# A two-layer decoder trunk: the first units' weight transfers tied to rows of the output projection, the modulation's columns tied to the units, and another order of the start

## The chip, the cores and the metric

The kernel runs on one core of one Trainium2 chip. The metric is the device time of one execution, in microseconds (us), as the median of several runs. All data are float32; a matmul takes its operands as "fp32r" pieces, high and low part, and each product is made of three matmuls (high x high, high x low, low x high).

## What is computed

Cut to what matters here:

```python
for i in range(DEPTH):                                  # 2 layers
    mod = (c_act @ ada_w[i] + ada_b[i])[:, None, :]     # 6 x 1024 columns
    sh1, sc1, g1, sh2, sc2, g2 = jnp.split(mod, 6, axis=-1)
    h = rmsnorm(x, norm1_g[i]) * (1.0 + sc1) + sh1
    proj = h @ w_in[i]
    mix = three mixers of proj                          # state space, pooling, attention
    x = x + g1 * (mix @ w_out[i])
    h = rmsnorm(x, norm2_g[i]) * (1.0 + sc2) + sh2
    x = x + g2 * conv_ffn(h, ffn_up[i], ffn_conv_w[i], ffn_conv_b[i], ffn_down[i])
return rmsnorm(x, final_g)
```

`x` is 1024 positions x 1024 channels, the hidden width of the gated MLP is 2816. `rmsnorm` divides by the root of the mean square over the channels, so it needs the whole sum of squares ("the root") before anything behind it can be made.

## The kernel before, in words

The channels lie on the partitions: `x` is eight tiles of 128 channels x 1024 positions. A helper library for tiles assigns buffers and semaphores, and its scheduler writes down each engine's order of instructions: by priority (the order of the program) among what its own model of time holds to be ready. Each engine then runs its list in order, and so does each queue of transfers: SP and ACT issue plain ones, POOL those that add to their destination (`accum_op=ALU.add`). `after(ins, dep)` (line 78) adds an edge that only fixes the order; with `sync` it is a real wait.

**The start.** `START` (line 32) is a list written by hand, and `start` (line 276) does one entry after the other: `x` loads the residual, `c`, `h`, `w` load data for the scale, the shift and the first weights, `S` adds up squares on ACT and DVE, `C` makes the scale (sixteen matmuls of one row, then a small transpose), `R0` the root in columns (line 198: matmuls L203, then L176 to L180), `R1` its spread over the positions (L211) and a copy into `xrs`, `X` multiplies half of `x` by it, `H` makes columns of the shift on DVE (L308), `M` and `N` the normalised input in high and low parts. The first projection (`vproj`, L411 to L413) follows.

**The columns of the modulation.** `ada_col` (line 138) makes one column of 128 values: two loads of 128 x 512 on SP (L142) into a ring of two raw buffers, which also serves the weights, and two multiply-and-add-up instructions on DVE (L143). Twelve columns are called for in the channel mixer of layer 0, one behind each of the units 7 to 18, and the rest among the down projection.

**The output projection, second part.** `accum_last` (line 1233) walks over two halves of 512 positions. In each, for eight blocks `n` of 128 channels: twelve matmuls into `dn` (L232 to L234), `accum` adds the result to the residual on DVE (L1211, called a row here), `store` writes it out on ACT's queue (L894), `square_add` squares it on ACT (L186) and adds it to `acc`, on POOL for n < 7 and on DVE for n = 7 (L187). The weights of a block are loaded on SP (L267) and split by ACT and DVE in the first half; those of n > 3 (`wkeep`, L261 and L262) are kept for the second. Behind each half come the root (L203) and its spread (L211). The seven first products of the channel mixer (`begin`, px and pv, L969 to L971) follow the second half.

**The units.** The channel mixer's up projection is done by a scheme of seven products in place of eight for each of 22 units (`unit`). A unit needs weights and sums of weights: `prepare(f)` (line 1018) loads S1 to S4 and A22 on SP (L989), and adds to them by transfers on POOL (L1024): S1 += w, S3 += w, S2 += S1, S4 += S2. Units 0 and 1 are prepared ahead of `accum_last`: ten loads that wait for `group_last`, the last addition of the projection's first part. Their eight sums are kept in a list, and `sums` issues one in each of the program's steps of the second half. `finish(f)` makes the convolution, the gate and the product on DVE (L1137, L1178) and writes it out.

## Time and profile before

| | us |
|---|---|
| median of 3 runs (2285.11 to 2291.4) | 2290.52 |
| the profiled execution, its own time | 2287.57 |
| its span, first to last instruction | 2285.8 |
| PE busy in the span | 2225.1 |
| DVE busy | 1553.3 |
| ACT busy | 1057.5 |
| POOL busy | 243.4 |

The engines are PE (matmul; PEld is its load of weights), DVE (vector), ACT (scalar functions), POOL (general) and SP (which issues transfers). A busy PE need not be PE at full speed: the granted clock is a column of its own, PEclk. A row of a timeline gives start, length, engine, line, operation, out<-in by the program's names, shapes and, in brackets, the idle time of the engine ahead of it with what ended that.

### The profile page before, as it was taken

The numbers are of one execution on the slowest core, as the hardware profiler recorded it, in microseconds if no ns is written. First come the engines' busy times: TensorE is split into PE (matmuls) and PEld (weight loads), VectorE is DVE, ScalarE is ACT, GpSimd is POOL, SyncE is SP. The second block draws the span as 40 slices with busy tenths as digits, with TensorE's granted clock in tenths as the row PEclk, the third lists the DMA queues.
The fourth block names the chain that finished last, engine by engine and source line by source line (L and its number), as shares of the span: only waits on it lengthen the run. The fifth ranks groups of instructions, "written<-read, shape, count | busy, mean of one in ns | idle before, by whom it ended". The sixth has DMA issues, their size and how long they took to land. (4 is left out here: it accounts for less than half of the span.)

```text
span 2285.8 us, 29760 instructions
## 1 busy us (share of the span) xinstructions
PE 2225.1 (97%) x10472; PEld 1808.7 (79%) x10472; DVE 1553.3 (68%) x2712; ACT 1057.5 (46%) x1960; POOL 243.4 (11%) x308
## 2 busy tenths in 40 slices
PE   6999999999999999999999999998999999999998
PEld 4878877778788888788888888776888888878887
DVE  6467888588766667995564567775966666675446
ACT  5366664355454445312234667533645455442212
POOL 0210000231111110000001000003211111100000
PEclk9999999999999999999999999999999999999999
DMA  7452333658876776991133221236777777663112
GB/s 275 130 146 79 93 112 126 164 161 221 212 197 172 179 175 202 338 298 59 56 134 108 56 56 48 87 106 183 181 179 174 175 175 179 162 244 106 47 47 88
DMA packets 186229, 338.94 MB, mean 148 GB/s; under 512 B 28704, under 2 KB 44320, under 8 KB 186080
## 3 DMA queue, kind: packets, MB, share of 16 engines
q1 hardware_dynamic: 126144, 244.44, 32.8%
q0 software_dynamic: 30560, 61.56, 15.0%
q10 hardware_dynamic: 29376, 31.05, 4.1%
q8 instruction: 82, 1.34, 0.2%
q14 instruction: 67, 0.55, 0.1%
HBM read 265.93 MB, written 44.83 MB: 136 GB/s over the span
## 5 line engine op out<-in xcount | busy, mean ns | idle before, releaser
L161 ACT CAST whi<-wraw 128x512 fp32r<-128x512 f32 (+2 forms) x196 | 117.6, 602 | 394.6 <-PE dq L233 274.1
L232 PE MATMUL dq<-ah,whi 128*128 128x512 f32 x576 | 227.0, 394 | 1.8 <-DVE xd L1230 1.4
L233 PE MATMUL dq<-al,whi 128*128 128x512 f32 x576 | 226.8, 394 | 0.0
L234 PE MATMUL dq<-ah,wlo 128*128 128x512 f32 x576 | 226.0, 393 | 0.0
L161 ACT CAST whi<-S 128x512 fp32r<-128x512 f32 x176 | 108.7, 619 | 206.9 <-PE px L970 129.0
L162 DVE TENSOR_TENSOR wlo<-wraw,whi 128x512 fp32r<-128x512 f32 (+2 forms) x196 | 129.8, 665 | 103.9 <-ACT whi L161 99.2
L1230 DVE SCALAR_TENSOR_TENSOR xd<-dq,mod,xd 128x1024 f32<-128x1024 f32 x80 | 102.7, 1284 | 123.8 <-PE dq L234 123.8
L162 DVE TENSOR_TENSOR wlo<-S,whi 128x512 fp32r<-128x512 f32 x176 | 124.5, 707 | 80.7 <-ACT whi L161 78.5
L143 DVE SCALAR_TENSOR_TENSOR araw<-araw,cact 128x512 f32<-128x512 f32 x160 | 106.1, 689 | 52.2 <-DMA araw<-in_adaw 51.8
L969 PE MATMUL px<-T24h,whi 128*128 128x512 f32 x352 | 138.9, 395 | 2.6 <-ACT s L1046 2.6
L971 PE MATMUL px<-T24h,wlo 128*128 128x512 f32 x352 | 138.3, 393 | 1.9 <-DVE wlo L162 1.9
L970 PE MATMUL px<-T24l,whi 128*128 128x512 f32 x352 | 138.5, 393 | 0.1
L969 PE MATMUL pv<-B,whi 128*128 128x512 f32 x344 | 135.7, 394 | 0.0
L970 PE MATMUL pv<-B,whi 128*128 128x512 f32 x344 | 135.6, 394 | 0.0
L971 PE MATMUL pv<-B,wlo 128*128 128x512 f32 x344 | 135.3, 393 | 0.0
L232 PEld LDWEIGHTS dq<-ah,whi 128*128 128x128 f32 x576 | 108.3, 188 | 28.0 <-issue 1.9
L1137 DVE SCALAR_TENSOR_TENSOR fg<-G,pff,fg 128x1023 f32<-128x1023 f32 x88 | 112.7, 1281 | 24.4 <-ACT fg L1135 24.3
L234 PEld LDWEIGHTS dq<-ah,wlo 128*128 128x128 f32 x576 | 108.4, 188 | 25.0 <-DVE wlo L162 0.5
L161 ACT CAST whi<-A 128x512 fp32r<-128x512 f32 x118 | 72.5, 615 | 118.9 <-PE pv L970 58.0
L233 PEld LDWEIGHTS dq<-al,whi 128*128 128x128 f32 x576 | 108.5, 188 | 23.9
L162 DVE TENSOR_TENSOR wlo<-A,whi 128x512 fp32r<-128x512 f32 x118 | 80.9, 686 | 63.8 <-ACT whi L161 59.5
L1024 POOL DMA_DIRECT2D S<-S x88 | 75.9, 871 | 430.2 <-DMA S<-in_up 284.2
(403 smaller groups left out, 5891.0 us busy)
## 6 DMA issues: line engine op xcount, KB each, us to landing
S<-in_up SPq DMA_DIRECT2D x176, 256.0 KB, 3.0
araw<-in_adaw SPq DMA_DIRECT2D x160, 256.0 KB, 4.2
A<-in_up SPq DMA_DIRECT2D x118, 256.0 KB, 3.6
S<-in_up POOLq DMA_DIRECT2D x88, 256.0 KB, 5.3
S<-S POOLq DMA_DIRECT2D x88, 256.0 KB, 4.0
raw<-act_d SPq DMA_DIRECT2D x88, 256.0 KB, 3.8
act_d<-fg SPq DMA_DIRECT2D x40, 512.0 KB, 3.6
wraw<-in_down SPq DMA_DIRECT2D x80, 256.0 KB, 2.7
```

The source lines that it names most:

```text
L143: dve.scalar_tensor_tensor(r, r, 1.0, cact[:, HALF[i]], ALU.mult, ALU.mult, accum_out=mod[l][:, j:j + 1] if i == 0 else mod2[:, j % 8:j % ...
L161: act.copy(hi[:, 0:n], raw)
L162: dve.tensor_tensor(lo[:, 0:n], raw, hi[:, 0:n].bitcast(F32), op=ALU.subtract)
L232: mm(ps, wh, hi[k][:, s], start=i == 0, stop=False)
L233: mm(ps, wh, lo[k][:, s], start=False, stop=False)
L234: mm(ps, wl, hi[k][:, s], start=False, stop=i == n - 1)
L969: after(mm(ps, wh[:, c], h_, start=first and k == 0, stop=False, skip_group_check=not first), dep)
L970: mm(ps, wh[:, c], l_, start=False, stop=False, skip_group_check=not first)
L971: mm(ps, wl[:, c], h_, start=False, stop=k == 3, skip_group_check=not first)
L1024: add = lambda: nc.gpsimd.dma_start(t, src, accum_op=ALU.add)
L1137: dve.scalar_tensor_tensor(acc[:, s:T], t[:, 0:T - s], pff[:, (2 - s) * 44 + cc:(2 - s) * 44 + cc + 1], acc[:, s:T], ALU.mult, ALU.add)
L1230: group_last[0] = dve.scalar_tensor_tensor(x[n], ps, mod[l][:, gcol + n:gcol + n + 1], x[n], ALU.mult, ALU.add)
```

## The change

Three edits. (1) In `START`, `R0 R1 X0` move ahead of `C0 H0`. (2) `ada_col` takes an instruction `dep`, behind which its DVE instructions are put in order; in the units it is the last product of `finish` (`fg_last`). (3) `prepare(0)` and `prepare(1)` are called from `sums` at block 6 of the first half, and their loads wait for that block's row; the sums are issued behind POOL's addition of squares of blocks 2 (S1 and S3 of both units), 4 (S2) and 6 (S4) of the second half. The other lines of the diff hand the instructions through.

```diff
--- before.py
+++ after.py
@@ -29,7 +29,7 @@
          "q3 n1 v0 q3 n1 q1 v1")
 
 
-START = "x0 x1 c0 h0 w0 S0 S1 C0 R0 R1 H0 X0 M0 c1 h1 w1 C1 H1 N1"
+START = "x0 x1 c0 h0 w0 S0 S1 R0 R1 X0 C0 H0 M0 c1 h1 w1 C1 H1 N1"
 WP4 = 8 * 132
 
 RING = ("ex",) * 6 + ("pm", "pt") * 2 + ("xd", "bc", "th") * 2
@@ -135,13 +135,13 @@
     act.activation(ccol, ccol, AF.Silu)
     act.activation(cact, cact, AF.Silu)
 
-    def ada_col(l, j, take=None):
+    def ada_col(l, j, take=None, dep=None):
 
         for i in range(2):
             r = take("araw") if take else rawp.tile([128, 528], F32, tag="raw", name="araw")[:, 0:512]
             nc.sync.dma_start(r, adaw_d[l, j, :, HALF[i]])
-            dve.scalar_tensor_tensor(r, r, 1.0, cact[:, HALF[i]], ALU.mult, ALU.mult,
-                                     accum_out=mod[l][:, j:j + 1] if i == 0 else mod2[:, j % 8:j % 8 + 1])
+            after(dve.scalar_tensor_tensor(r, r, 1.0, cact[:, HALF[i]], ALU.mult, ALU.mult,
+                                           accum_out=mod[l][:, j:j + 1] if i == 0 else mod2[:, j % 8:j % 8 + 1]), dep)
         if j % 8 == 7:
             s = slice(j - 7, j + 1)
             dve.tensor_tensor(mod[l][:, s], mod[l][:, s], mod2, op=ALU.add)
@@ -184,7 +184,7 @@
             return act.activation(acc, t, AF.Square)
         sq = p2("sq", "nh", 3)[:, 0:acc.shape[-1]]
         r = act.activation(sq, t, AF.Square)
-        eng.tensor_tensor(acc, acc, sq, op=ALU.add)
+        square_last[0] = eng.tensor_tensor(acc, acc, sq, op=ALU.add)
         return r
 
     def rstd(acc, n, tab):
@@ -211,7 +211,7 @@
             spread_last[0] = mm(ps[:, b * 128:(b + 1) * 128], r[:, b:b + 1].to_broadcast([128, 128]), ident, start=True, stop=True)
         return ps[:, 0:nb * 128]
 
-    spread_last = [None]
+    spread_last, square_last = [None], [None]
 
     def modulate(l, which, k, hs, rs, hi, lo):
         t = p2("ht", "nh", 3)[:, 0:rs.shape[-1]]
@@ -1005,27 +1005,27 @@
                     units[f].V1 = pb("pv", ("ps", "ps", "po")[f])
                     product(units[f].V1, raw, "B21", True, spread_last[0] if i == 3 else None, w)
 
-        pending = []
-
-        def sums(part, n):
-
-            if part and pending and n < 7:
-                pending.pop(0)()
-                if n == 6:
-                    while pending:
-                        pending.pop(0)()
-
-        def prepare(f):
+        def sums(part, n, row, sq):
+
+
+            if not part and n == 6:
+                for f in (0, 1):
+                    prepare(f, row)
+            elif part and n in (2, 4, 6):
+                for f in (0, 1):
+                    for t, src in units[f].sums[{2: slice(0, 2), 4: slice(2, 3), 6: slice(3, 4)}[n]]:
+                        after(nc.gpsimd.dma_start(t, src, accum_op=ALU.add), sq)
+
+        def prepare(f, dep=None):
 
             u = units.setdefault(f, Unit())
-            dep = group_last[0] if f < 2 else None
+            u.sums = []
 
             def plus(t, src):
-                add = lambda: nc.gpsimd.dma_start(t, src, accum_op=ALU.add)
                 if f < 2:
-                    pending.append(add)
+                    u.sums.append((t, src))
                 else:
-                    add()
+                    nc.gpsimd.dma_start(t, src, accum_op=ALU.add)
 
             if f > 3:
                 u.A11 = up_w("A11", f, 0)
@@ -1143,8 +1143,6 @@
 
         minus = pff[:, 0:132].rearrange("p (s c) -> p s c", s=3)[:, :, NFF:2 * NFF]
         dve.tensor_scalar(minus, minus, -1.0, None, op0=ALU.mult)
-        prepare(0)
-        prepare(1)
         accum_last(wout_d[l, 1], ys, 16, l, None, PARTS[0], first_half, begin, second_half, store, sums)
 
         todo = [(0, 40 + k) for k in range(8)] + [(1, p * 8 + k) for p in (1, 0, 2, 4, 3, 5) for k in range(8)] if l == 0 else []
@@ -1152,7 +1150,7 @@
         def ada(n, take=None):
             for _ in range(n):
                 if todo:
-                    ada_col(*todo.pop(0), take)
+                    ada_col(*todo.pop(0), take, None if take else fg_last[0])
 
         def acts(fs, pool):
             out = []
@@ -1167,7 +1165,7 @@
             return out
 
 
-        si = None
+        si, fg_last = None, [None]
 
         def finish(f):
             nonlocal si
@@ -1175,7 +1173,7 @@
             g = conv(p.G, f, "fg")
             u = conv(p.U, NFF + f, "fu")
             si = act.activation(g, g, AF.Silu)
-            dve.tensor_tensor(g, g, u, op=ALU.mult)
+            fg_last[0] = dve.tensor_tensor(g, g, u, op=ALU.mult)
             (nc.sync if f < NFF - 2 else nc.gpsimd).dma_start(act_d[f], g)
 
         for f in range(NFF + 1):
@@ -1208,7 +1206,7 @@
     cnt_, group_last = [0], [None]
 
     def accum(ps, n, hs, gcol, l):
-        dve.scalar_tensor_tensor(x[n][:, hs], ps, mod[l][:, gcol + n:gcol + n + 1], x[n][:, hs],
+        return dve.scalar_tensor_tensor(x[n][:, hs], ps, mod[l][:, gcol + n:gcol + n + 1], x[n][:, hs],
                                  ALU.mult, ALU.add)
 
     def acc_ps():
@@ -1244,12 +1242,12 @@
                     then(n, *done)
                 ps = acc_ps()[:, 0:hs.stop - hs.start]
                 gemm(ps, w[n], mh, ml, hs, range(4))
-                accum(ps, n, hs, gcol, l)
+                row = accum(ps, n, hs, gcol, l)
                 if store:
                     store(n, hs)
                 square_add(acc, x[n][:, hs], n == 0, nc.gpsimd if rest and n < 7 else dve)
                 if sums:
-                    sums(hs.start, n)
+                    sums(hs.start, n, row, square_last[0])
                 if done and not early:
                     then(n, *done)
             done = hs, rstd_spread(*rstd_begin(acc, D, "pt", tab))
```

## The prediction, written before the changed kernel was run

> **What bounds the kernel now.** I read the page's busy times first, then PE's list of waits over the whole span (what waited, for what, us in total, times, longest):
>
> ```profile
> PE 2225.1 (97%) x10472; PEld 1808.7 (79%) x10472; DVE 1553.3 (68%) x2712; ACT 1057.5 (46%) x1960; POOL 243.4 (11%) x308
> ...
> PE scrow L314 <- DMA sraw<-in_adas: 17.2, 2, 16.8
> PE ssps L203 <- DVE acc L187: 11.8, 3, 8.1
> PE dn L232 <- ACT wkeep L261: 4.6, 2, 2.8
> ...
> PE px L971 <- DVE wlo L162: 1.9, 1, 1.9
> PE px L970 <- DVE T13l L910: 1.8, 2, 1.4
> ```
>
> PE is busy for 97% of the span, so only time in which PE stands, or runs at half clock, is to be won. Of its waits the first is the start. The second and third belong to the two passes of the output projection, one in each layer, and the rest to the units of the channel mixer. Next I timed those two passes with the windows view, limited to tile dn, from the first dn matmul to the one after the last (192 matmuls each), and took single rows from PE's timeline, where the bracket is the idle time ahead of the row:
>
> ```profile
> 421.81:478.19 56.38, 48.86 (x192) 38.13 (x191) 11.08 (x15) 0.91 0.69 195
> 1536.35:1595.68 59.33, 47.04 (x192) 36.74 (x191) 11.20 (x15) 0.91 0.64 184
> 441.41 0.80 PE L232 MATMUL dn<-yh,wkeep 128*128 128x512 f32 x1 [2.80 <-ACT wkeep L261]
> ...
> 454.10 1.40 PE L203 MATMUL ssps<-ones,acc 128*128 128x1 f32 x8 [2.10 <-DVE acc L187]
> ...
> 467.08 0.40 PE L232 MATMUL dn<-yh,wkeep 128*128 128x512 f32 x1
> ...
> 478.19 0.40 PE L969 MATMUL px<-B,whi 128*128 128x512 f32 x1
> ...
> 481.86 0.95 PE L203 MATMUL ssps<-ones,acc 128*128 128x1 f32 x8
> ...
> 484.38 1.05 PE L211 MATMUL ssps<-ident,rcol 128*128 128x128 f32 x8
> ```
>
> ```profile
> 1554.94 0.50 PE L232 MATMUL dn<-yh,wkeep 128*128 128x512 f32 x1 [1.81 <-ACT wkeep L261]
> ...
> 1572.40 1.87 PE L203 MATMUL ssps<-ones,acc 128*128 128x1 f32 x8 [8.10 <-DVE acc L187]
> ```
>
> The undisturbed pitch is (478.19 - 467.08)/48 = 0.2315 us, since four output blocks of 12 matmuls lie between these rows. 192 of them take 44.4 us, and the root's two groups (0.95 and 1.05) bring it to 46.4. Layer 0's pass took 56.38 and layer 1's 59.33: 10.0 and 12.9 us are lost. Visible idle is 2.80 + 2.10 = 4.90 and 1.81 + 8.10 = 9.91; the other 5.1 and 3.0 are matmuls at half clock behind the pauses (in a row of the windows view stand PE, PEld, DVE, ACT and POOL busy, then PEclk, DMA share and GB/s):
>
> ```profile
> 441.00:444.20 3.20, 2.79 (x7) 2.17 (x8) 1.24 (x2) 1.50 (x3) 0.79 (x2) 0.50 0.49 131
> ...
> 456.00:461.00 5.00, 5.00 (x17) 4.28 (x16) 0.62 (x4) 0.66 (x2) 0.44 (x1) 0.50 0.64 157
> ...
> 1554.90:1557.00 2.10, 2.06 (x8) 1.41 (x9) 1.79 (x3) 1.15 (x2) 0.00 (x0) 1.00 1.12 210
> ```
>
> After 2.80 idle the granted clock is 0.50 for three us, and it is 0.50 again after 2.10; after 1.81 it is 1.00. [...]
>
> **What causes the pauses.** SP's and ACT's timelines in layer 0:
>
> ```profile
> 432.60 2.19 SPq L267 DMA_DIRECT2D wraw<-in_wout  x2
> 440.74 0.62 ACT L261 CAST wkeep<-wraw 128x512 fp32r<-128x512 f32 x1 [3.60 <-DMA wraw<-in_wout]
> 436.51 0.63 ACT L186 ACTIVATE sq<-xx 128x512 f32<-128x512 f32 x1 [3.13 <-DMA xf_d<-xx]
> ```
>
> The last two pieces of the output weights (L267, issued at 432.60 and later) stand on SP's queue behind the ten loads of units 0 and 1, and land among them: ACT can cast one only at 440.74, and PE stands 2.80. ACT's row at 436.51 shows a second effect: a square waits 3.13 for the store of the residual ahead of it on ACT's queue. The long wait of the root (8.10) is POOL's, seen in its timeline in layer 1:
>
> ```profile
> 1566.78 0.87 POOL L1024 DMA_DIRECT2D S<-S  x1 [4.54 <-issue]
> 1567.38 4.24 POOL L187 TENSOR_TENSOR acc<-acc,sq 128x512 f32<-128x512 f32 x3
> ```
>
> POOL stands 4.54 ahead of a sum (the profile names only "issue"; the sum that this one reads was issued before it, and such a one takes about 4.3 to land, below), and only then does three additions of squares in a row. The root needs the last of them.
>
> **The first units' transfers: both passes.** The change lets the ten loads wait for row 6 of the first half (estimate: 421.81 + 84 x 0.2315 + 1 = 442.3 in layer 0) and ties the sums behind POOL's additions 2, 4 and 6 of the second half. What it removes: the loads from in front of the last output weights (2.80 and 1.81 idle) and every sum from the first half's additions (2.10 and 8.10), with the half-clock time behind them. What stands behind the new wait on SP is the units' loads themselves and, at worst, the seven pieces for the first products, wanted only after 478. What is late next is the last addition of the first half on DVE: the root sits 11 matmuls (2.5 us) behind the half's end, and in the second half, where nothing blocks it, it sits 481.86 - 478.19 = 3.7 behind and does not wait. So 0 to 1.2 us of idle per layer remain, too short to halve the clock by the 1.81 row. Do the sums still come in time? The median landings near the first pass are:
>
> ```profile
> S<-in_up SPq DMA_DIRECT2D x9, 256.0 KB, 6.9
> ...
> S<-in_up POOLq DMA_DIRECT2D x4, 256.0 KB, 7.2
> S<-S POOLq DMA_DIRECT2D x4, 256.0 KB, 4.3
> ```
>
> 442.3 plus a load (6.9) is 449, ahead of addition 2 of the second half (estimate: 444 for the end of the first half, three blocks of 2.8, 2.0 for the root and 2 for the row and its square, 456). The sums add 7.2 + 4.3 + 4.3, so the last lands near 472, and some microseconds later with two units' sums in line. In the undisturbed time PE ends the pass at 421.8 + 46.4 = 468 and does seven products of 12 (19.4 us), to 488, before it needs a sum. If those 16 us of cover were gone, PE would stand for each microsecond over it. I take 2 us of the loss as left per layer, between 0 and the 5 of the rival below: 22.9 - 4 = 18.9 gained (12.9 to 22.9).
>
> **The paced columns.** Layer 0's units have 24 half columns of the modulation between them. DVE's waits between 480 and 640, a PE row and three windows:
>
> ```profile
> DVE araw L143 <- DMA araw<-in_adaw: 22.0, 9, 5.9
> 598.27 0.51 PE L971 MATMUL px<-T24h,wlo 128*128 128x512 f32 x1 [1.91 <-DVE wlo L162]
> 560.00:600.00 40.00, 38.09 (x165) 30.66 (x164) 26.44 (x48) 16.22 (x25) 5.21 (x6) 1.00 0.88 231
> 600.00:640.00 40.00, 37.38 (x161) 29.84 (x160) 31.55 (x45) 19.77 (x30) 7.40 (x9) 1.00 0.81 213
> 640.00:680.00 40.00, 40.00 (x175) 32.57 (x174) 25.45 (x32) 20.21 (x30) 8.03 (x10) 1.00 0.73 185
> ```
>
> DVE stands 22.0 us for column data, in order, ahead of the units' own work; the addition that PE wants then comes late (1.91 idle at 598.27). Full windows hold 175 matmuls (640:680), those before it 165 and 161: 24 x 0.2315 = 5.6 us lost. Layer 1 has no columns here, and its longest wait of the T13l kind is 0.4 against 1.4 (the row above: two waits, 1.8), so 0.9 more. The change puts each column behind the product of an earlier unit from unit 7 on: two half columns per unit, whose data come well ahead, so DVE does not stand for them. DVE is busy 25.45 of 40 in 640:680 and has room. Gain between 0, if the same waits return there, and 6.5; I take 5.
>
> **The first norm's root.** Rows of the start:
>
> ```profile
> 10.77 9.21 DVE L289 TENSOR_TENSOR xacc<-xacc,xsq 128x1024 f32<-128x1024 f32 x7 [0.99 <-ACT xsq L287]
> ...
> 26.44 1.95 PE L203 MATMUL ssps<-ones,xacc 128*128 128x1 f32 x16
> ...
> 31.23 3.65 PE L211 MATMUL ssps<-ident,rcol 128*128 128x128 f32 x16 [1.86 <-DVE rcol L180]
> ...
> 35.53 4.63 DVE L330 TENSOR_TENSOR x<-x,xrs 128x1024 f32<-128x1024 f32 x4 [0.47 <-ACT xrs L327]
> 25.00:30.00 5.00, 4.37 (x28) 2.99 (x26) 3.28 (x7) 1.46 (x6) 0.00 (x0) 1.00 1.00 395
> 30.00:35.00 5.00, 3.77 (x17) 3.44 (x18) 3.79 (x16) 1.83 (x4) 0.00 (x0) 0.66 1.05 393
> ```
>
> The sum of squares is done at 19.98, yet the root's matmuls run at 26.44: in PE's order they stand behind the sixteen of the scale (C0), which wait for data (the 17.2 of the first list). The change puts root and spread ahead of C0, so the normalisation on DVE (35.53, 4.63) can begin up to 26.44 - 19.98 = 6.5 earlier, at 29. But DVE has most of that stretch filled: its free time from 25 to 35 is (5 - 3.28) + (5 - 3.79) = 2.9, and part of it waits for data. Against that, C0's matmuls and with them the scale come later by up to the root's two groups on PE, 1.95 + 3.65 less the 1.86 of idle that they can use, 3.7. I bound the whole by -2 (3.7 less what the earlier root gives DVE) and +2.9, and take +1, nearer to the unused DVE time.
>
> **Sum.** 18.9 + 5 + 1 = 25 us off the profiled execution: 2287.57 - 25 = 2262.6. The median of the runs, 2290.52, is 2.95 above that execution, so the forecast for the median is 2265.5, written 2265.
>
> **Rivals.** First, the stores take the place of the output weights: as the ACT row at 436.51 showed, an ACT store issued among the ten loads holds the square behind it about 3 us. The loads now start at row 6, and the store of row 7 follows 2.8 us later, so the last square, the root and PE could be 2 to 3 late, with 5 us at half clock behind it as after layer 0's second pause (456 to 461, half of it lost): 5 per layer. The gain is then 12.9 + 5 + 1 = 18.9: 2271.6. For it: the queue behind the loads is the same. Against: the output weights and the sums no longer share the transfers. Chance 0.17.
>
> Second, the columns wait in their new place as they did in the old: 2265.5 + 5 = 2270.5. Chance 0.10.
>
> Third, the ties only move the waits: POOL's additions of the second half stand behind its sums and the second root, which did not wait, now does. At the first half's price the 18.9 are given back and 5 + 1 = 6 stay: 2284.5, no change that can be told. POOL's issues now fall where DVE is fullest:
>
> ```profile
> 490.00:500.00 10.00, 10.00 (x45) 8.10 (x44) 10.00 (x13) 4.29 (x9) 3.56 (x4) 1.00 0.44 121
> ...
> 495.97 0.87 POOL L1024 DMA_DIRECT2D S<-S  x1 [4.13 <-DVE xx L916]
> ```
>
> With DVE busy 10.00 of 10, a POOL issue takes 0.87. [...] Chance 0.08.
>
> Fourth, slower: the chain load, sum, sum, sum is too slow for unit 0. If every link took twice its median (13.8 + 14.4 + 8.6 + 8.6 = 45.4) and four of POOL's additions stood 4.54 behind a sum, as at 1566.78, the last sum would land at 442.3 + 45.4 + 18.2 = 506. PE would stand from 488 to 506, 18 us, with 2.5 of half clock behind it: 41 in two layers against 25 gained, 2290.5 + 16 = 2306.5. It makes the kernel slower from about 14 us of standing per layer. The medians speak against it. Chance 0.05.
>
> That the change does nothing is possible for the root alone, if C0 still runs first on PE; that is inside the range.
>
> **Chances.** The forecast has 0.60, so 0.60 + 0.17 + 0.10 = 0.87 for faster by over 0.3% (6.9 us, about what a measurement of this kernel can tell from no change), 0.08 within it, 0.05 slower. The range: best bounds 22.9 + 6.5 + 2.9 = 32.3 give 2258.2, with a little room 2257; the worst of the first two rivals with the start at -2, 12.9 + 0 - 2 = 10.9, give 2279.6, with room 2281. It leaves the third and fourth rivals out.
>
> **What would show it.** Right: no load of units 0 and 1 on SP's queue before row 6; no PE wait for wkeep in either pass; the passes last 47 to 49 us; POOL's first-half additions follow ACT's squares at once; no araw wait on DVE between 480 and 615 and 175 matmuls in each 40 us there; the root's matmuls near 20. Wrong: a PE wait at the root of over 2 us with clock 0.50 behind it; a wait for a unit's S ahead of its first T2 product; araw waits after 640; the first projection later than 41.8.

## The result, and the profile after

The changed kernel takes 2277.27 us (median of 4 runs, 2276.12 to 2278.41) against 2290.2 for the kernel before on the same chip: ratio 0.9945, 95% interval 0.9926 to 0.9964. It is faster by 12.9 us, half of the 25 us that were forecast; the sign is right and the time lies in the range, well off the value. Its profiled execution took 2276.12 us, with a span of 2274.3.

First the page's busy times of the changed kernel, and then PE's list of waits (what waited, for what, us in total, times, longest):

```profile
PE 2224.9 (98%) x10472; PEld 1809.5 (80%) x10472; DVE 1557.3 (68%) x2712; ACT 1060.5 (47%) x1961; POOL 244.6 (11%) x308
```

```profile
PE ssps L203 <- DVE acc L187: 8.0, 3, 3.7
...
PE px L970 <- DVE T13l L910: 1.4, 1, 1.4
```

The waits for `wkeep` are gone. The root's wait is not: 8.0 in three waits where it was 11.8 in three (one of 1.6, behind the last down projection, stands in both). The two passes of the output projection, in the windows view limited to tile dn, and then the same view of all instructions for the time behind each:

```profile
428.31:474.49 46.18, 44.89 (x192) 35.75 (x191) 10.78 (x15) 1.00 0.66 197
1529.92:1575.99 46.07, 44.77 (x192) 35.75 (x191) 10.46 (x14) 1.00 0.63 199
```

```profile
481.00:487.00 6.00, 6.00 (x22) 5.32 (x23) 1.59 (x5) 1.70 (x4) 0.85 (x1) 0.51 0.97 223
1583.50:1590.00 6.50, 6.42 (x24) 5.77 (x24) 1.62 (x5) 1.08 (x3) 0.85 (x1) 0.51 0.88 190
```

Both passes now run undisturbed, with the clock at 1.00, in 0.2 and 0.3 us less than the 46.4 that the forecast worked out as the ideal. Right behind each, the clock is 0.51 for six microseconds. PE's timeline shows why:

```profile
474.49 0.40 PE L969 MATMUL px<-B,whi 128*128 128x512 f32 x1
...
480.96 1.70 PE L203 MATMUL ssps<-ones,acc 128*128 128x1 f32 x8 [2.64 <-DVE acc L187]
...
1583.58 1.81 PE L203 MATMUL ssps<-ones,acc 128*128 128x1 f32 x8 [3.71 <-DVE acc L187]
```

The second root, which did not wait before, now stands 2.64 and 3.71 us. Cutting both profiled executions at the same matmuls gives the balance (us):

| stretch | before | after | won |
|---|---|---|---|
| start to the first score product (qk) | 66.4 | 70.5 | -4.1 |
| from there to layer 0's pass | 355.4 | 357.8 | -2.4 |
| pass, layer 0 | 56.4 | 46.2 | +10.2 |
| first 84 matmuls of the units, layer 0 | 21.3 | 27.3 | -6.0 |
| rest of the up projection, layer 0 | 415.2 | 408.2 | +6.9 |
| down projection and layer 1 to its pass | 621.7 | 619.9 | +1.9 |
| pass, layer 1 | 59.3 | 46.1 | +13.3 |
| first 84 matmuls of the units, layer 1 | 21.4 | 28.4 | -7.1 |
| rest of the up projection, layer 1 | 408.6 | 409.7 | -1.2 |
| all that follows | 260.2 | 260.1 | 0 |

The sum is 11.5, the difference of the spans. The gain of the passes came in full (23.5), and 13.1 of it were given back within the 168 matmuls behind them; the start lost instead of winning.

### The profile page after: what moved, and what is told of

The parts are those of the page before. It is cut to its first block, busy times and chain, and to the rows that moved or that the text cites. A ratio compares the mean times of both kernels' runs of the same rounds, so it can differ in the third digit from the quotient of the medians.

```text
span 2274.3 us, 29754 instructions
## 1 busy us (share of the span) xinstructions
PE 2224.9 (98%) x10472; PEld 1809.5 (80%) x10472; DVE 1557.3 (68%) x2712; ACT 1060.5 (47%) x1961; POOL 244.6 (11%) x308
## 4 chain that ended last, share of the span: by engine, by line
PE 93%; DVE 3%; DMA 2%; ACT 1%; issue 1%; ACTq 0%; DVEq 0%; SPq 0%
PE px L970 7%; PE px L969 7%; PE dq L232 7%; PE px L971 7%; PE dq L233 7%; PE dq L234 7%; PE pv L970 5%; PE pv L969 5%; PE pv L971 5%; PE dn L234 2%; PE dn L233 2%; PE dn L232 2%; PE qk L232 1%; PE qk L233 1%; PE qk L234 1%; PE z L232 1%
## 5 line engine op out<-in xcount | busy, mean ns | idle before, releaser
L232 PEld LDWEIGHTS dq<-ah,whi 128*128 128x128 f32 x576 | 108.2, 188 | 28.2 <-issue 2.0
L1137 DVE SCALAR_TENSOR_TENSOR fu<-U,pff,fu 128x1023 f32<-128x1023 f32 x88 | 112.3, 1276 | 0.1
```

Source lines behind the costliest of these rows:

```text
L232: mm(ps, wh, hi[k][:, s], start=i == 0, stop=False)
L1137: dve.scalar_tensor_tensor(acc[:, s:T], t[:, 0:T - s], pff[:, (2 - s) * 44 + cc:(2 - s) * 44 + cc + 1], acc[:, s:T], ALU.mult, ALU.add)
```

## The experiments

All are edits of the changed kernel. Each was timed beside the kernel before on its own chip, and the ratio to that is what compares across chips. The changed kernel run again (c1) shows how well it repeats.

> The changed kernel itself, a second time, on the chip of the three that follow, so that they are read against it. Both theories: 2277 us; how far its executions lie apart tells what a difference of 3 us between two kernels is worth.

Measured: 2279.86 us, ratio 0.9959 (0.9945 to 0.9973); its root waits 3.9 and 4.0. The same kernel thus differs by 0.0014 of the time, 3.2 us, between two chips; a smaller difference between kernels timed on different chips shows nothing.

### The start

`s1` restores the old order, `s2` and `s3` restore one half of it each, in `START`:

```diff
-... S0 S1 R0 R1 X0 C0 H0 M0 ...
+... S0 S1 C0 R0 R1 H0 X0 M0 ...    (s1)
+... S0 S1 R0 R1 C0 H0 X0 M0 ...    (s2)
+... S0 S1 C0 R0 R1 X0 H0 M0 ...    (s3)
```

> The changed kernel with the start's order of the kernel before (the condition's columns, then the first norm's root, then half 0's columns and the scale-and-shift), all else as changed. Theory start: the new order costs 4.1 us by the end of the first projection and 2.2 us more at half clock behind the idle time at 120 to 124 us, so this kernel is 6.5 us faster than the changed one, about 2270.8 us; the last product of the first projection ends near 66.3 us and not 70.4. Rival (the forecast's own sum): the new order is worth 1 us, and this kernel takes about 2278 us; the 6.5 us would then come from something else that the order does not touch.

> The changed kernel with the start's order root, condition's columns, half 0's columns, scale-and-shift: the root stays ahead of the columns on the matrix engine, only the scale-and-shift goes back behind half 0's columns. Theory A (the columns' matmuls are cut up by the root's and end at 33.8 us): the delay stays, first projection ends at 69 to 70.5 us and the time is 2276 to 2278 us. Theory B (the scale-and-shift stands ahead of half 0's columns on the vector engine and waits 2.66 us for the root while the columns' data lie ready): most of the delay goes, first projection ends near 67 us, time 2271 to 2273 us.

> The changed kernel with the start's order condition's columns, root, scale-and-shift, half 0's columns: the columns' matmuls are whole again, the scale-and-shift stays ahead of half 0's columns on the vector engine. Theory A (cut-up columns): most of the delay goes, first projection ends near 67 us, time 2271 to 2273 us. Theory B (order on the vector engine): the delay stays, first projection ends at 69 to 70.5 us, time 2276 to 2278 us.

Measured: 2277.02 (0.9944, 0.9928 to 0.9961), 2278.59 (0.9951, 0.9937 to 0.9966) and 2275.3 (0.9937, 0.9924 to 0.9951) us. The first score product starts at 68.2, 71.6 and 66.6. PE's timeline at the start, of the changed kernel, of s2 and of s3:

```profile
17.16 1.86 PE L314 MATMUL scrow<-sraw,ccol 128*1 128x512 f32 x2 [17.16 <-ACT xsq L287]
20.18 3.54 PE L203 MATMUL ssps<-ones,xacc 128*128 128x1 f32 x16 [1.16 <-DVE xacc L289]
23.66 1.87 PE L314 MATMUL scrow<-sraw,ccol 128*1 128x512 f32 x2
25.45 1.95 PE L211 MATMUL ssps<-ident,rcol 128*128 128x128 f32 x8
27.33 1.02 PE L314 MATMUL scrow<-sraw,ccol 128*1 128x512 f32 x2
28.28 1.16 PE L211 MATMUL ssps<-ident,rcol 128*128 128x128 f32 x8
29.37 4.45 PE L314 MATMUL scrow<-sraw,ccol 128*1 128x512 f32 x10
```

```profile
20.31 3.54 PE L203 MATMUL ssps<-ones,xacc 128*128 128x1 f32 x16 [1.38 <-DVE xacc L289]
...
30.54 4.45 PE L314 MATMUL scrow<-sraw,ccol 128*1 128x512 f32 x10
```

```profile
17.14 9.13 PE L314 MATMUL scrow<-sraw,ccol 128*1 128x512 f32 x16 [17.14 <-DMA sraw<-in_adas]
26.20 1.95 PE L203 MATMUL ssps<-ones,xacc 128*128 128x1 f32 x16
```

With the root ahead, the sixteen matmuls of the scale are cut into four groups and end at 33.8 (29.37 + 4.45) and 35.0; in s3 they end at 26.3, as before the change. DVE's rows of the changed kernel show what that does:

```profile
30.10 4.63 DVE L330 TENSOR_TENSOR x<-x,xrs 128x1024 f32<-128x1024 f32 x4 [2.66 <-ACT xrs L327]
...
38.30 0.15 DVE L155 SCALAR_TENSOR_TENSOR acol<-mod,par 128x4 f32<-128x4 f32 x1
```

The normalisation starts at 30.10, 5.4 earlier than before, after a stand of 2.66 in which no column of the shift is made; the scale is ready at 38.30, and before it was ready at 30.69. So the root came early, and the scale, which the first projection needs as well, came 7.6 late: 5.3 by PE (the scale's first step on DVE, L152, is at 35.77 and was at 30.48), and the rest by DVE's list, which puts a column of the shift and two splits of weights ahead of L155. The theory of the cut-up matmuls holds: s3 is early and s2 late. The rival about DVE's order is not excluded as a part of it, because s2 still has the 2.65 us stand ahead of the normalisation and s3 executes on DVE in the order of the kernel before: the scheduler makes DVE's order follow PE's.

Over all profiles of this study but s2 and s3, which move one half of the order each, the first score product starts at 65.8 to 68.2, mean 67.3, in the eight with the old order, and at 68.7 to 72.0, mean 70.6, in the ten with the new: 3.3 us, not the 6.5 that I took from one profile. The further 2.4 up to the pass (357.8 against 355.4) come with more time at half clock between 119 and 178: three steps of 3.41 us, where the kernel before has one. Five of the ten profiles with the new order show three such steps and take 357.8 to 358.8; the eight with the old order show one or two and take 355.3 to 356.8. Whether the order makes them likelier is open.

The lateness does not reach the projection's start. The modulation on ACT (L334) needs the normalised `x` and the scale; rows of the kernel before, then of the changed one:

```profile
30.69 0.16 DVE L155 SCALAR_TENSOR_TENSOR acol<-mod,par 128x4 f32<-128x4 f32 x1
...
36.79 2.38 ACT L334 ACTIVATE xt<-x,mod,acol 128x1024 f32<-128x1024 f32 x2 [1.29 <-DVE x L330]
44.62 0.57 ACT L316 COPY scr<-scrow 1x512 f32<-1x512 f32 x1
45.24 1.05 PE L319 MATMUL sccol<-ones,scr 1*128 1x1 f32 x8
```

```profile
38.49 2.38 ACT L334 ACTIVATE xt<-x,mod,acol 128x1024 f32<-128x1024 f32 x2 [1.69 <-DVE acol L155]
46.31 0.57 ACT L316 COPY scr<-scrow 1x512 f32<-1x512 f32 x1
46.94 1.26 PE L319 MATMUL sccol<-ones,scr 1*128 1x1 f32 x8 [1.25 <-ACT scr L316]
```

ACT starts 1.70 later, and so copies the row of the scale's second half (L316) 1.69 later. PE has the second sixteen matmuls of the scale to do first and begins the projection at 42.42 (41.77 before), but in the middle of it stands 1.25 for that copy, and the clock is 0.50 in the window 47.7 to 50.9 behind the pause. From its first matmul to the first score product the projection takes 24.6 to 24.8 us in the eight profiles with the old order and in s3, which have no such pause; 28.0 to 28.2 in s2 and in eight of the ten with the new order; and 26.6 and 26.7 in t4 and t2, which have the pause and no half clock behind it. That is where the order's cost lies.

In time, s1 alone does not show it: its runs lie between 2271.5 and 2281.96, and its expectation of 2270.8 was missed, as was the 2271 to 2273 of the better theory for s3. Pairs on one chip agree with the marks, below: 4.8 and 3.9 us.

### The columns

```diff
-                    ada_col(*todo.pop(0), take, None if take else fg_last[0])
+                    ada_col(*todo.pop(0), take)
```

> The changed kernel with the modulation's columns not tied to the units. Theory: the pacing is worth the 5.3 us that layer 0's units win between their 84th and 504th products, so this kernel is 5 us slower than the changed one, about 2282 us, and the matrix engine waits again in the window from 510 to 625 us. Rival: the units' time there is set by something else (the late second root only moved it) and this kernel takes the changed one's time within 1 us, 2277 us.

Measured: 2284.93 us (0.9971, 0.9959 to 0.9983). Its expectation was 2282. In its profile DVE again stands 22.5 us for column data between 480 and 640, and the 1000th matmul of layer 0's units comes 245.4 us behind the pass, in the changed kernel 239.5. The pacing is worth 5.9 us there (in time 2.7 to 6 us, by the ratios 0.9971 against 0.9959 and 0.9945, whose intervals overlap; the marks of o1 against s1, below, give 5.1). The windows of the changed kernel, where 165 and 161 matmuls ran before:

```profile
560.00:600.00 40.00, 40.00 (x175) 32.48 (x174) 24.82 (x31) 19.96 (x30) 6.85 (x8) 1.00 0.71 181
600.00:640.00 40.00, 40.00 (x175) 32.49 (x174) 27.61 (x39) 19.59 (x29) 6.83 (x8) 1.00 0.78 192
```

### The second root

Two theories. T1: POOL is late, because its last additions of squares stand behind sums and their landings. T2: DVE is late, its row 7 and last addition. POOL's and DVE's timelines of the changed kernel (layer 0, the pass ends at 474.49):

```profile
465.61 1.30 POOL L187 TENSOR_TENSOR acc<-acc,sq 128x512 f32<-128x512 f32 x1 [1.43 <-ACT sq L186]
466.85 3.54 POOL L1017 DMA_DIRECT2D S<-in_up  x4
469.30 4.11 POOL L187 TENSOR_TENSOR acc<-acc,sq 128x512 f32<-128x512 f32 x2
473.37 0.83 POOL L1017 DMA_DIRECT2D S<-S  x1
475.67 0.85 POOL L1017 DMA_DIRECT2D S<-S  x1 [1.47 <-DMA S<-in_up]
476.25 3.42 POOL L187 TENSOR_TENSOR acc<-acc,sq 128x512 f32<-128x512 f32 x2
479.61 0.84 POOL L1017 DMA_DIRECT2D S<-S  x1
```

```profile
476.75 0.74 DVE L1209 SCALAR_TENSOR_TENSOR xx<-dn,mod,xx 128x512 f32<-128x512 f32 x1
477.41 1.13 DVE L902 SCALAR_TENSOR_TENSOR B<-xx,mod,B 128x512 fp32r<-128x512 f32 x1
478.46 1.75 DVE L910 TENSOR_TENSOR wkeep<-wraw,wkeep 128x512 fp32r<-128x512 f32 x1
480.14 0.68 DVE L187 TENSOR_TENSOR acc<-acc,sq 128x512 f32<-128x512 f32 x1
```

Row 7 in the kernel before, where the pass ended at 478.19:

```profile
478.62 0.73 DVE L1211 SCALAR_TENSOR_TENSOR xx<-dn,mod,xx 128x512 f32<-128x512 f32 x1
```

Both are late: POOL's last addition ends at 479.67, and DVE's row 7 starts 2.26 behind the pass (0.43 in the kernel before). DVE also has operations of 1.13 and 1.75 us where their kind takes 0.74 and 0.68. Here DVE's last addition (480.14) starts 0.47 behind POOL's. In c1, the same kernel, it does not wait for POOL, which is done at 476.79, and row 7 starts 4.97 behind the pass (472.29):

```profile
473.49 3.30 POOL L187 TENSOR_TENSOR acc<-acc,sq 128x512 f32<-128x512 f32 x2
```

```profile
477.26 0.74 DVE L1209 SCALAR_TENSOR_TENSOR xx<-dn,mod,xx 128x512 f32<-128x512 f32 x1
...
479.18 0.68 DVE L187 TENSOR_TENSOR acc<-acc,sq 128x512 f32<-128x512 f32 x1
```

So either engine can be the last, from one execution of a kernel to the next.

`t1` leaves the eight sums out; `t2`, `t3`, `t4` and `t5` move them (only the line that changes the rows is shown, with a comment of mine; the next lines give each sum its row):

```diff
-            elif part and n in (2, 4, 6):     # S1 and S3; S2; S4
+            elif part and n == 6:             # t2: all of them behind row 6
+            elif part and n in (0, 2, 4):     # t3
+            elif part and n in (2, 6):        # t4: S1 and S3; S2 and then S4
+            elif part and n in (1, 4, 6):     # t5
```

> The changed kernel without the eight summing transfers of units 0 and 1 in each layer (this part of the computation is left out: those sums of pieces are not formed). Theory T1 (GpSimd is late with the second half's last additions of squares because it issues the sums and waits for their landings): the second root's waits of 2.64 us and 3.71 us and the half clock behind them vanish, the first 84 products behind each output projection take 21.3 us again and not 27.3 and 28.4, and the time is 10 to 14 us under the changed kernel's, about 2265 us. Theory T2 (VectorE is late: it is busy without a gap from 457 to 480 us and its last square comes 2.26 us behind the last product): the waits stay at 2 us or more and the time within 3 us of the changed kernel's.

> The changed kernel with all eight sums of units 0 and 1 behind the second half's last addition of squares on GpSimd. Theory T1: the second root no longer waits (under 1 us), but the chain of sums starts some 5 us later and the first product that reads the third sum would be late; with sums of 4 to 9 us from issue to landing that wait is 0 to 6 us a layer, so the time is 2265 to 2278 us. Theory T2: the root's waits stay at 2 us or more in both layers and the time is 2276 us or more.

> The changed kernel with the sums of units 0 and 1 tied to rows 0, 2 and 4 of the second half and not 2, 4 and 6. Theory T1 (what delays the root is the last two sums, issued between GpSimd's last additions): the root's waits fall under 1 us and the time falls by 8 to 14 us, to about 2266 us. Theory T2 (VectorE's backlog): waits of 2 us or more stay. A third case: the second sum's landing, 4 to 9 us behind its issue, holds GpSimd in the middle of the half instead, and the waits shrink only by half: 2271 us.

> The changed kernel with the first sums of units 0 and 1 behind row 2 as it has them, and the second and third sums both behind GpSimd's last addition of the second half (row 6). The late sums showed a wait of 6 us for T24h in place of the root's. Theory T1: GpSimd then holds only four issues (2.6 us) among its additions, so the root's wait is 0 to 1.5 us; the third sums come 2 us later than in the changed kernel, and the first product that reads T24h waits 1 to 3 us: 2272 to 2278 us. If the wait for T24h is as long as with all sums late (6 us), 2285 us.

> The changed kernel with the sums tied to rows 1, 4 and 6 and not 2, 4 and 6: only the first sums go, by one row. By the trace of the changed kernel the loads that they read have landed at 461 us, before row 1's addition ends at 464.2 us. Theory T1: the four first issues run in GpSimd's idle time between rows 1 and 2, the second sums find the first landed, and the root's waits fall under 1 us with the third sums no later than now: 8 to 11 us less than the changed kernel, about 2267 us. If the loads are not there yet (as with row 0), GpSimd stands at the first sum and the time is 2277 to 2281 us.

Measured, with the root's two waits, the start of DVE's row 7 behind the end of the pass, and how far DVE's operations of over 0.95 us in the second half exceed 0.74 together (layer 0 / layer 1, us):

| kernel | median | ratio to before (95%) | root waits | row 7 behind | DVE excess |
|---|---|---|---|---|---|
| before | 2290.2 | 1 | 0 / 0 | 0.4 / 0.6 | 1.5 / 1.5 |
| changed | 2277.27 | 0.9945 (0.9926 to 0.9964) | 2.6 / 3.7 | 2.3 / 2.8 | 3.4 / 4.3 |
| t1, no sums | 2269.07 | 0.9901 (0.9887 to 0.9915) | 0.3 / 0.6 | 1.1 / 1.4 | 1.5 / 0.8 |
| t2, all behind row 6 | 2285.2 | 0.9973 (0.9964 to 0.9982) | 0 / 0 | 0.8 / 0.4 | 0.8 / 0.8 |
| t3, rows 0, 2, 4 | 2280.78 | 0.9955 (0.9941 to 0.9968) | 2.8 / 4.1 | 3.9 / 5.3 | 2.9 / 3.2 |
| t4, rows 2, 6, 6 | 2272.72 | 0.9935 (0.9916 to 0.9954) | 1.7 / 2.7 | 2.4 / 3.9 | 2.4 / 3.4 |
| t5, rows 1, 4, 6 | 2279.72 | 0.9956 (0.9942 to 0.997) | 2.4 / 2.8 | 3.5 / 1.5 | 3.7 / 3.4 |

PE's waits in t1 and then in t2, in layer 0 around the end of the pass:

```profile
PE ssps L203 <- DVE acc L187: 0.3, 1, 0.3
```

```profile
PE px L969 <- ACT T24h L906: 6.1, 2, 5.9
```

Without sums the first 84 matmuls of the units take 21.9 and 22.1 us again: the sums cause 11.8 of the 13.1 us lost there. That is what T1 expected of the waits; the time is 10.8 us under c1's on the same chip. But t2 shows that they can't simply go later: the root is free, and the product that needs the third sum stands 6 us in each layer, the wait of the forecast's fourth rival. Nor can they go earlier: in t3, for which T1 expected 2266 and the slowest of its three cases 2271, the loads have not landed, POOL stands in front of the sums (4.91 us ahead of the last of the first four), the additions pile up behind it, and the passes themselves grow to 49.7 and 48.7. t4 takes the middle way and is 7.1 us under c1 on its chip (its executions spread over 13 us; e2 against e1, below, shows 6.5 for the same move with intervals apart), yet its root still waits; t5, for which T1 expected 2267, is a plain miss. In t5 POOL's last addition ends 3.0 us behind layer 0's pass, where it was 5.2, and the root waits almost as long. So T1 alone does not hold, and the stretched operations come in. POOL's and DVE's timelines in t5:

```profile
474.75 3.33 POOL L187 TENSOR_TENSOR acc<-acc,sq 128x512 f32<-128x512 f32 x2
```

```profile
474.84 2.08 DVE L902 SCALAR_TENSOR_TENSOR B<-xx,mod,B 128x512 fp32r<-128x512 f32 x1
476.85 1.77 DVE L910 TENSOR_TENSOR wkeep<-wraw,wkeep 128x512 fp32r<-128x512 f32 x1
478.55 0.74 DVE L1209 SCALAR_TENSOR_TENSOR xx<-dn,mod,xx 128x512 f32<-128x512 f32 x1
```

POOL's two additions run from 474.75 to 478.08. DVE's L902 and L910 (each takes two inputs from SBUF) are stretched over them: L910 ends at 478.62, 0.54 behind POOL; then row 7 (L1209), with one input in PSUM, takes 0.74. In the changed kernel L1209 takes its 0.74 at 476.75 although an addition of POOL runs (476.25 to 479.67).

Three more kernels test this by moving the second half's additions of squares from POOL to DVE: for rows 5 and 6 in `e1` (sums as changed) and in `e2` (sums as in t4), for all of them in `b5` (sums as in t4, old start). The comments name the runs.

```diff
-                square_add(acc, x[n][:, hs], n == 0, nc.gpsimd if rest and n < 7 else dve)
+                square_add(acc, x[n][:, hs], n == 0, nc.gpsimd if rest and n < (5 if hs.start else 7) else dve)   # e1, e2
+                square_add(acc, x[n][:, hs], n == 0, nc.gpsimd if rest and not hs.start and n < 7 else dve)   # b5
```

> The changed kernel with the second half's additions of squares for rows 5 and 6 on VectorE and no longer on GpSimd; the sums as changed. If GpSimd's order alone makes the root late, the wait falls under 1 us, since nothing behind the third pair of sums is then needed by the root: about 2268 to 2270 us. If VectorE's own backlog does (its operations locked against GpSimd's earlier additions, 1.6 to 2.4 us in place of 0.74), two more additions of 0.68 us on it leave 1.5 to 3 us of wait: 2275 to 2279 us.

> The same two additions on VectorE, with the first sums behind row 2 and the others behind row 6. With fewer of GpSimd's additions beside VectorE's at the end of the half, VectorE's operations longer than 0.95 us should number one or two and not four, and the root's wait be under 1 us; the second sums can go as soon as the first have landed. If the locks are the cause: 2266 to 2270 us. If not, it equals the run with the sums split alone, 2272 to 2275 us.

> The start's order of the kernel before and the split sums, with all of the second half's additions of squares on VectorE. If GpSimd's additions are what stretches VectorE's operations, none of VectorE's operations there is longer than 0.95 us (four or five were, 3.3 us over 0.74 in all); VectorE gets six additions of 0.68 us, 4.1 us, so the last row's end moves by under 1 us, and GpSimd can start the second sums as soon as the first have landed. Root's wait 1 to 3 us, time 2267 to 2271 us. If something else stretches them, they stay, the last row comes 4 us later, the root waits 5 us or more, and the time is 2276 us or more.

Measured: e1 2280.62 us (0.9953, 0.994 to 0.9967), root waits 1.8 and 2.8; e2 2274.08 (0.9926, 0.9914 to 0.9939), 1.6 and 1.3; b5 2275.34 (0.9936, 0.9923 to 0.9949), none. In e1 POOL's last addition ends 1.0 to 1.2 us ahead of the end of the pass, and the root still waits: what is left is DVE's backlog (row 7 at 2.7 and 2.9 behind), as T2 had it. Both expectations for e1 were below its time. That of e2 was missed too: it had set 2266 to 2270 and a wait under 1 us for the case that the stretched operations are the cause, and 2272 to 2275 for the case that they are not, and 2274 came. It does not decide between them, because two operations in each layer stay stretched (2.0 us in all) and DVE has taken over two more additions. b5 takes the stretching away altogether. DVE's L902 in the second half, by groups (count, then busy us and mean ns), in the changed kernel and in b5:

```profile
L902 DVE SCALAR_TENSOR_TENSOR B<-xx,mod,B 128x512 fp32r<-128x512 f32 x8 | 8.2, 1038 | 0.0
```

```profile
L902 DVE SCALAR_TENSOR_TENSOR B<-xx,mod,B 128x512 fp32r<-128x512 f32 x8 | 5.9, 746 | 1.5 <-ACT B L901 1.5
```

With no addition on POOL the mean falls from 1038 to 746 ns, and not one of DVE's operations there exceeds 0.95 us. In b2 (below), the same kernel as b5 but for these additions, four in each layer do, 3.3 and 3.4 us over 0.74 together, and the root waits 2.9 and 2.7. In b5 the root does not wait. This is the sign that b5's expectation had set for the stretching by POOL's additions; its time, 2267 to 2271, was missed, for DVE now carries six more additions of 0.68, and PE's waits in b5 lie inside the pass:

```profile
PE dn L232 <- DVE xx L1210: 3.4, 3, 2.1
```

The passes last 50.3 and 49.5 us. So in every run with sums inside the second half, wherever the additions stood, DVE and POOL together came through that half a little later than an unhindered PE, which needs 24 us for it. In t1 and t2, with no sums ahead of the last addition, the root waits 0.6 or less.

### The parts together

`b1` is s1 with t3, `b3` s1 with t5, `b2` s1 with t4, `b4` s1 with e2; `o1` is s1 with p1, so that the ties alone are left.

> The start's order of the kernel before and the sums tied to rows 0, 2 and 4: both suspected costs away together. If they are the two costs and add up (6.5 us at the start, 8 to 14 us at the two second roots), 2257 to 2263 us. If T2 holds, the start's share alone, 2271 us. If neither, 2277 us.

> The start's order of the kernel before, and the sums tied to rows 1, 4 and 6. If the start costs the 3.7 us by which its profiles show the first scores' transpose earlier, this is 3 to 5 us under the run with rows 1, 4 and 6 alone, and about 2263 us if that one gives 2267. If the start's order is worth nothing in the end, it equals that run within 1.5 us.

> The start's order of the kernel before, and the first sums behind row 2, the others behind row 6. The start was worth 3.3 to 4.8 us between pairs of kernels on one chip; the split sums 7 us. If they add, 2267 to 2269 us, 10 us under the changed kernel; if not, 2272 us.

> The start's order of the kernel before, the first sums behind row 2 and the others behind row 6, and the second half's additions of squares of rows 5 and 6 on VectorE. If the start's 4 us add to the run without it (2274), 2270 us; no more than 1 us from the kernel with the additions left on GpSimd, since the root's wait stays at 1.3 to 1.6 us.

> The ties alone: the start's order of the kernel before and the columns without their tie. By the marks of the traces the ties win 23.5 us in the two output projections and give back 14 us in the units behind them, 9 us in all: 2281 us, and the run with the tie of the columns off (2285) less the start's 3.7 us says the same. The forecast's first term alone (18.9 us) would give 2271 us.

Measured: b1 2276.01 us (0.994, 0.9928 to 0.9952), 4.8 under t3 on its chip; b3 2275.81 (0.994, 0.9926 to 0.9955), 3.9 under t5 on its chip; b2 2269.44 (0.9908, 0.9894 to 0.9922); b4 2270.77 (0.9915, 0.99 to 0.9929); o1 2281.02 (0.9957, 0.9945 to 0.997). Put back, the old start is worth about 4 us in these two pairs; the intervals of each pair overlap, and the comparisons across chips (s1, b2 and b4 against the changed kernel, t4 and e2) give 0 to 6. b2, with the old start and the split sums, is the fastest kernel of the study that computes all: 22.4 us under the kernel before on its chip, about as much as had been forecast for the change itself, and it lies below the changed kernel too (0.9908 against 0.9945 and 0.9959, intervals apart). The ties alone win 10.8 us on their chip where the forecast's first term was 18.9.

## Why half of the predicted gain did not come

**Passes, 18.9 (12.9 to 22.9).** The passes were worth 23.5, above the upper bound, since they reached 46.2 and 46.1 and no microsecond was left of the 2 per layer. What should show it did: no wait for `wkeep`, the loads issued behind row 6 (SP's first at 448.68; row 6 ends at 448.65, 20.3 us into the pass, 20.5 forecast), POOL's first-half additions at once behind the squares. The first rival (stores among the loads) did not occur: no square waited for a store in the first half, and the root behind it did not wait. That a pause of 1.81 is too short to halve the clock, as the forecast had it, is no rule: the last section shows 1.73 that did.

**The step that failed** is the sentence "in the second half, where nothing blocks it, it sits 481.86 - 478.19 = 3.7 behind and does not wait". It took the second root's slack from a kernel in which the second half was slow: 448.65 to 478.19, 29.5 us, with the pauses of PE giving DVE and POOL time. The change itself takes the pauses away (24.0 us for the same work) and puts eight issues into POOL's second half, which had none. Both use up the slack: the root stood 2.64 and 3.71 us, with half clock behind it. The forecast had this as its third rival, at a chance of 0.08, with the mechanism right and the extent too large (all 18.9 given back): what was given back behind the passes is 6.0 and 7.1, 13.1 of 23.5, and without the sums (t1) 11.8 of it are gone. It looked at the row of a POOL issue beside a busy DVE (0.87; the four of S<-S in the changed kernel's layer 0 take 0.83 to 0.85), and not at POOL's additions beside DVE: in t5 L902 and L910 take 2.08 and 1.77 beside additions, and 0.74 and 0.68 without; in b5, with no addition on POOL in the second half, no operation of DVE there takes over 0.95. The fourth rival's wait, for the third sum, was absent in the change and appears in t2, 6 us in each layer.

**Columns, 5 (0 to 6.5).** Right: 5.9 by the marks with the pacing off. DVE's 22.0 us of standing for column data between 480 and 640 are gone, and one of 1.9 us is left later in the up projection, which PE does not notice. The second rival fell.

**Start, +1 (-2 to +2.9).** Wrong sign: -3.3 by the profiles, about -4 by the timed pairs. The estimate let the scale be late by at most 3.7, PE's time for the root and its spread less idle time. It is 7.6 late: PE stands 1.16 ahead of the root, and between its first and last matmul of the scale lie the root's 3.54 (not 1.95) and the spread's 1.95 + 1.16, of which nothing is hidden; together 7.8 us more. The earlier root did free the normalisation at 30.1 (29 forecast), but the modulation waits for the scale and starts 1.7 later than before. The forecast put the price on PE's time ahead of the projection, and it lies elsewhere: in the pause for ACT's copy within the projection and the half clock behind it. The forecast's own sign of failure, a first projection later than 41.8, appears (42.4), but it tells nothing: with the old order the projection starts anywhere between 41.1 and 43.4.

**Sum.** 23.5 - 13.1 for the ties, +6.9 for the rest of layer 0's units and -1.2 for that of layer 1's, -6.5 for the start up to the pass and 1.9 elsewhere make the 11.5 of the spans. The last three contain variation between executions: the stretch from the down projection to layer 1's pass takes 619.9 to 625.4 in the profiles taken, and the changed kernel's was the shortest. That the time lies in the range is luck as far as the sum goes: the range's slow end was made of the first two rivals, which did not occur, and left out the third, which did.

**Left open.** What is left of the root's wait in the split kernels (1 to 3 us) is shared between DVE's backlog and POOL's order in a way that no run separates fully, since an addition moved from one engine loads the other, and the engine that is last differs between executions of one kernel. Why s1's runs spread over 10 us was not found.

## What to carry to other kernels

A wait that "does not occur" was measured beside the other waits: when a change removes the pauses of the bounding engine, work out the helpers' load anew against the shorter stretch before counting the gain. Work that is tied to a place on a queue should be tried at several places, for too early it stands for its input, and too late its reader stands; here two rows made 7 us. And when something is moved ahead, follow what it delays to the same reader: the first projection needs the root and the scale, so an earlier root is worth nothing while the scale comes later, and the time can be lost further on, where a queue that started late keeps another engine standing.

## What the hardware showed that was not expected

In the passes of the kernel before and of the changed one, wherever an addition of POOL and a DVE operation with two SBUF inputs overlap by over 0.15 us, one of them takes longer than it does alone (1.30 and 0.68 to 0.75). DVE's L902 takes 0.74 or 0.75 without an addition beside it; beside one it takes up to 1.88 in the kernel before and in the changed one, and 2.08 in t5. L262 takes 2.52 once in the kernel before, and 0.68 or 0.69 the other five times in its passes; a pair of POOL's additions grows from 2 x 1.30 to 3.33 in t5. Around the two passes of these two profiles, fourteen of DVE's operations on 128x512 take over 0.95 us, all of them beside an addition: thirteen end 0.55 or 0.56 us behind the end of an addition, and for one (L902 at 1571.63 in the changed kernel, 1.56) the addition, itself 2.97 long, ends 1.13 behind it. It looks as if one runs when the other is done. The profile counts the longer time as busy (8.2 us for the eight of L902 in the changed kernel, 5.9 in b5), so DVE looks full and not delayed. The operations with an input in PSUM (the rows) keep their time: 35 of them overlap an addition in these passes, and they take 0.73 to 0.75. So does L902 beside POOL's issues of sums: three in the changed kernel, 0.74 each.

The pause that halves the clock can be shorter than the rows of the kernel before showed. In t4 PE's timeline and a window behind it read:

```profile
476.11 1.02 PE L203 MATMUL ssps<-ones,acc 128*128 128x1 f32 x8 [1.73 <-DVE acc L187]
...
477.33 0.63 PE L971 MATMUL pv<-B,wlo 128*128 128x512 f32 x1
```

```profile
477.20:480.20 3.00, 3.00 (x8) 2.08 (x7) 0.46 (x2) 0.80 (x3) 0.62 (x1) 0.51 1.05 249
```

After 1.73 us of idle time and the root's eight one-column matmuls the granted clock is 0.51, while 1.81 of idle time ahead of full-size matmuls in the kernel before left it at 1.00. The length of a pause thus does not decide. In the profiles of the kernel before and of the changed one the clock changes in steps: between 31 and 2260 us the stretches at half clock last 3.41, 6.83 or 10.24 us, and the changes lie whole multiples of 3.41 apart. Counted back from the change at 1567.39, a step ends at 1553.74, and the 1.81 of the kernel before lie across it (0.61 and 1.20). The 1.73 of t4 lie in one step by an estimate: with stretches of 3.41, the 0.51 of the 3.00 us window above puts the start of the half clock between 476.7 and 477.3, and the pause, from 474.38 to 476.11, into the 3.41 ahead of it.

In the passes and units of these two profiles (420 to 920 and 1520 to 2020 us), behind each of the five steps at full clock in which three or fewer matmuls of 512 columns start, the clock was half, and behind each with six or more it stayed full. PE's busy time alone does not decide: over the whole span the kernel before has a step (212.30 to 215.72) that is 100% busy, with matmuls of at most 192 columns, and was followed by half clock, and one (594.60 to 598.01) that is 52% busy, with six of 512, and was followed by full. Nor do the columns started, added up, separate the steps everywhere: 2062 (24.57 to 27.98) were followed by full clock and 2752 (1328.46 to 1331.87) by half. What decides is not shown. Where the steps fall differs between executions: 441.00 in the kernel before and 481.11 in the changed one lie 11.75 steps apart.
